# A two-layer attention and gated-MLP kernel: last-stage arithmetic moved from GpSimd to VectorE and ScalarE, weight splits tied to the last attention blocks, gates and first loads reordered

## The chip, the cores and the metric

The kernel runs on one core of a Trainium2 chip. The metric is the device time of one execution in microseconds (us), as the median of three runs. The engines are named as in the profile: PE (TensorE matmuls), PEld (its weight loads), DVE (VectorE), ACT (ScalarE), POOL (GpSimd) and SP (SyncE, which here issues most of the DMAs).

## What is computed

The input is a sequence of 2048 tokens of width 1024 and 256 context tokens. Two layers are applied, each followed by a residual and a layer norm:

```python
def even_layer(x, xc, c, c_ctx, ...):        # layer 0
    q_a, k_a, v_a, g_a, q_b, k_b, v_b, g_b = even_heads(modulate(x, shift, scale) @ w_in, ...)
    # 8 heads with low-rank q and kv (rms norms of rank 384 and 256) and a rope part,
    # 8 heads of 64 with 2 kv heads; keys are context + sequence
    y = attend_and_merge(...)                # softmax attention, times silu(gate), @ w_out
    x_new = layer_norm(ALPHA * x + gate * y, ln_g, ln_b)
def odd_layer(x, ...):                       # layer 1
    u, v, g = jnp.split(modulate(x, shift, scale) @ w_in, 3, axis=-1)
    v = layer_norm(jax.nn.gelu(v), v_ln_g, v_ln_b)
    # v is mixed over chunks of 128 tokens by w_s, then
    y = (jax.nn.gelu(u) * mixed * jax.nn.silu(g)) @ w_out
    x_new = layer_norm(ALPHA * x + gate * y, ln_g, ln_b)
```

All of it is float32. Every product of two matrices is made of three matmuls: each operand is split into a high part `h` (rounded to the type that TensorE reads at full rate) and a low part `l = x - h`, and h·h, h·l and l·h are summed in PSUM. A split is thus one copy with rounding and one subtraction over the tile; the weights are split on the chip too.

## The kernel before

There are three stages on one instruction stream per engine. A planner of the framework orders the instructions of each engine when the kernel is built, by program order as priority and by its own estimate of when each becomes ready; what is emitted under `tc.high_priority()` goes first. On the chip every engine runs its queue in that fixed order and waits on semaphores. In attention the order of PE, DVE, ACT and POOL is written out by hand (class `InOrder`, whose every instruction has line 588 in the profile).

**Stage 1, `phase1`.** First the modulation row: 16 loads of `e_w_mod` (512 KB each) feed matmuls of two rows (L118). The raw tiles of the context and of the first 512-token chunk are loaded between the third and the fourth group of these loads. Then come two halves, the first with the context and chunks 0 and 1, the second with chunks 2 and 3. `acts` scales a chunk's raw tiles on ACT (L165) and splits them on POOL (L167) and DVE (L168); `weights` loads a weight tile of 512 KB and splits it on POOL (L147) and DVE (L148); `gemm` makes 24 matmuls of 512 columns (L176 to L178). The split chunks stand in a ring of nine tile pairs. In each half there are the keys, values and queries of the second kind of head, the low-rank kv part, the low-rank q part (`w1[8]` to `w1[10]`, then a norm over 384 channels, `finish`, which I call the join of the query norm: square sums by a matmul L240, Sqrt L242, reciprocal, multiply, split), and the product with `uq`, which needs the join. The 16 units of the generator `gate` (`gates`, a `gemm`, a Silu L295 and a store to `G`) are put between these parts where the program calls `next(gate)`; what is left of them is run behind `uq`. In the second half those last gates run beside `first_peaks`: 28 units of one product and one row maximum (L603, L607, L617, L620) that find the largest score of each query for the first two attention blocks. The negated maxima of block 0 go to memory (`NM`) and come back as a row of the query tile (`peak_row`), and the first score product of attention reads that row.

**Stage 2, `attention`.** 64 blocks (16 heads by four groups of 512 queries) of 18 key tiles each. POOL adds the exponentials `ph` of most key tiles into a running sum (`sa`), for all blocks but the last four (`shares`); `total` splits the sum on ACT (`sh`) and POOL (`sl`). `sh` stands in ACT's hand-written order among the exponentials of the next block.

**Stage 3, `phase3`.** Four batches of 512 tokens. `even_out` is the out-projection, residual and norm of layer 0, with transposes L970 at its end; `odd_in` is the in-projection of layer 1: `v` (L978, ACT), then 16 column tiles `j`, eight for `u` and eight for `g`; `odd_out` is the last projection (its PSUM tiles are emptied by L1046) with the norm L948 and L949. PSUM tiles `acc` are a ring of six, of which a half of a projection fills four. Weights are split on ACT (L65) and DVE (L66). The first three weight tiles, `pre`, are split on POOL instead (L62, L63, through `split(..., pool=True)`) and may run as soon as they are loaded. For a `g` tile, ACT makes the Silu into an SBUF tile `y` (L1019) and POOL multiplies it into `u` (L1020). POOL also turns the normalized residual `T` into `T * eg + eb` in eight instructions of 128x1024 a batch (L1032), which may run when the transposes have read `T`.

Of the kernel before, what the change touches and what calls it, by code (L numbers as in the profile page):

```python
# [54 lines left out]
    e.eps = e.epsq[1.0]  # L55


def split(e, h, l, src, pool=False):

    if pool:  # L60
        pool = e.nc.gpsimd if pool is True else pool
        pool.tensor_scalar(out=h, in0=src, scalar1=1.0, scalar2=0.0, op0=ALU.mult, op1=ALU.add)  # L62
        pool.tensor_tensor(out=l, in0=src, in1=h.bitcast(F32), op=ALU.subtract)  # L63
    else:
        e.nc.scalar.activation(h, src, AF.Copy)  # L65
        e.nc.vector.tensor_tensor(out=l, in0=src, in1=h.bitcast(F32), op=ALU.subtract)  # L66


def phase1(e):
    nc, tc, I = e.nc, e.tc, e.ins  # L70
    early = ExitStack()
    with tc.tile_pool(name="p1c", bufs=1) as cp, tc.tile_pool(name="p1", bufs=2, reuse_waits="tile") as sp, \
# [28 lines left out]
        def raws(c, kk, tag="xr", bufs=2):  # L101
            src = I["ctxT"] if c < 0 else I["xT"][:, c * CH:(c + 1) * CH]
            src = src.rearrange("(k p) t -> p k t", p=P)
            r = sp.tile([P, 2, CH], F32, name="xr", tag=tag, bufs=bufs)
            nc.sync.dma_start(r[:, :, :CTX if c < 0 else CH], src[:, 2 * kk:2 * kk + 2, :])
            return r
# [4 lines left out]
        for j in range(4):  # L111
            ps = pp.tile([P, CH], F32, name="ps", tag="ps", bufs=5)
            for kk in range(4):
                tag, bufs = ring[(4 * j + kk) % 8]
                w = sp.tile([P, 2, CH], F32, name="wr", tag=tag, bufs=bufs)
                nc.sync.dma_start(w, I["e_w_mod"].rearrange("(k p) f -> p k f", p=P)[:, 2 * kk:2 * kk + 2, j * CH:(j + 1) * CH])
                for k in range(2):
                    nc.tensor.matmul(ps[:2, :], lhsT=sc[:, 2 * kk + k, :], rhs=w[:, k, :],  # L118
                                     start=kk + k == 0, stop=kk + k == 4)
            mrow = ap.tile([2, CH], F32, name="mrow", tag="sq", bufs=4)  # L120
            nc.scalar.activation(mrow, ps[:2, :], AF.Copy)
            for i in range(4):
                nc.tensor.transpose(mps[:, 4 * j + i, :], mrow[:, i * P:(i + 1) * P], e.ident[:2, :2])
            if j == 2:

                raw = {(c, kk): raws(c, kk, "xl", 9) for c in (-1, 0) for kk in range(4)}
        md = cp.tile([P, 2, 16], F32, name="md")
        for c in range(2):
            nc.vector.tensor_tensor(out=md[:, c, :], in0=mps[:, :, c], in1=bmod, op=ALU.add)
# [6 lines left out]
        def weights(src, shape):  # L136
            for f in aside[:rate]:
                f()
            del aside[:rate]
            w = sp.tile([P, 1024], F32, name="wr", tag="wr", bufs=2)  # L140
            n = 1
            for s in shape[1:]:
                n *= s
            nc.sync.dma_start(w[:, :n], src)
            h = sp.tile([P, 1024], F32R, name="wh", tag="wh", bufs=3)
            l = sp.tile([P, 1024], F32R, name="wl", tag="wl", bufs=3)
            nc.gpsimd.tensor_scalar(out=h[:, :n], in0=w[:, :n], scalar1=1.0, scalar2=0.0, op0=ALU.mult, op1=ALU.add)  # L147
            nc.vector.tensor_tensor(out=l[:, :n], in0=w[:, :n], in1=h[:, :n].bitcast(F32), op=ALU.subtract)  # L148
            if len(shape) == 3:
                return tuple(t[:, :n].rearrange("p (a b) -> p a b", a=shape[1]) for t in (h, l))  # L150
            return tuple(t[:, :n].rearrange("p (a b c) -> p a b c", a=shape[1], b=shape[2]) for t in (h, l))
# [128 lines left out]
        for half in range(2):  # L280
# [172 lines left out]

                        queue.append(finish)

            next(gate)
            for s in range(3):
                w = weights(I["uq"][s], [P, 2, 3, P])
                for i in range(2):
# [20 lines left out]
                todo = first_peaks(e, sp, pp)  # L480
            for i, _ in enumerate(gate):
                if half == 1 and i > 0:
                    for f in todo[:7]:
                        f()
                    del todo[:7]
            assert not aside
        flush()
        for f in todo:
# [144 lines left out]
def first_peaks(e, sp, pp):  # L633

    nc, (K, _), Q = e.nc, e.first[0], e.first[1]
    e.stats, pms = {}, {}

    def one(i, m):
        peak_products(e, nc.tensor, pp, pms, (0, i), i, K, Q[i], m, "misc", 3)
        peak_maxima(e, nc.vector, e.kp, pms, e.stats, i, m)  # L640

    return [lambda i=i, m=m: one(i, m) for i, n in ((0, NTT), (1, AHEAD)) for m in range(n)]


def attention(e):
# [8 lines left out]
    with tc.tile_pool(name="atc", bufs=1, reuse_waits="tile") as cp, \  # L654
# [135 lines left out]
        def at(time, *unit):  # L790
            units.append((time, len(units), unit))

        stats.update(e.stats)
        for i in range(NW):
            if i > 1:
                at((i - 2) * NTT + 1.2, fetch_queries, i)
            if i % NG == 1 and i // NG + 1 < 2 * NH:
                at(i * NTT + 1.2, fetch_keys, i // NG + 1)
            for m in range((NTT, AHEAD)[i] if i < 2 else 0, NTT):
                at(i * NTT - NTT - AHEAD + m + 0.6, peak, i, m)  # L800
                at(i * NTT - NTT - AHEAD + m + 1.3, top, i, m)
            at(max(0, i * NTT - AHEAD + 2.5) - (i == 0), row, i)
        for s in range(NW * NTT):
            i, t = divmod(s, NTT)
            parts, adds = shares(i)
# [25 lines left out]
        at(end - (NG - 2) * NTT + 1, lambda: z_load(e, 0, e.Z[0].groups[3]))  # L831
        for k in range(NK):
            at(end - (NG - 1) * NTT + 4 * k + 17, lambda k: z_split(e, e.Z[0][k], sp.tile([P, CH], F32, name="zt", tag="zt", bufs=2), POOL), k)
        for _, _, (f, *args) in sorted(units):
            f(*args)


def phase3(e):
    nc, tc, I = e.nc, e.tc, e.ins
    NB = SEQ // CH  # L840
    with tc.tile_pool(name="p3c", bufs=1, reuse_waits="tile") as cp, \
# [41 lines left out]
        def wtile(q):  # L883
            return wp.tile([P, 1024], F32R if q else F32, name="w" + q, tag="w" + q, bufs=3 if q else 2)

        def weights(src, a, hl=None, w=None, pool=False):
            w = w or wtile("")
            nc.sync.dma_start(w.rearrange("p (a b) -> p a b", a=a), src)
            h, l = hl or (wtile(q) for q in "hl")
            with tc.high_priority():  # L890
                split(e, h, l, w, pool)
            return tuple(t.rearrange("p (a b) -> p a b", a=a) for t in (h, l))

        def residual(b, T, q):
# [80 lines left out]
        def odd_in(b, X, Z, T, v):  # L975
# [28 lines left out]
            for j in range(16):  # L1004
# [7 lines left out]
                if j < 8:  # L1012
                    if j % 2 == 0:
                        u = sp.tile([P, 2, CH], F32, name="u", tag="u", bufs=4)
                        U += [u[:, i, :] for i in range(2)]
                    nc.scalar.activation(U[j], ps, AF.Gelu_apprx_tanh)
                else:
                    y = tmp("y", 3)
                    nc.scalar.activation(y, ps, AF.Silu)  # L1019
                    nc.gpsimd.tensor_tensor(out=U[j - 8], in0=U[j - 8], in1=y, op=ALU.mult)  # L1020
                    if j > 8:
                        gated(j - 9, st)
                    mixed(j - 8, st)
# [5 lines left out]
                        z_load(e, b + 1, Z.groups[j], nc.gpsimd)  # L1029
                if 4 <= j < 12:  # L1030
                    t = (j - 4) // 2
                    nc.gpsimd.tensor_tensor(out=T[:, t, :], in0=T[:, t, :], in1=C["eb" if j % 2 else "eg"], op=ALU.add if j % 2 else ALU.mult)  # L1032
            gated(7, st)
            return U

# [4 lines left out]
        def odd_out(b, Z, T):  # L1040
            xr = [T[:, t, :] for t in range(4)]

            def evac(t, cc, ps):
# [8 lines left out]
            token_major(Z, I["o_w_out"], 0, evac, stagger=b == NB - 1)  # L1052


        pre = [weights(I["e_w_out"].rearrange("(k p) f -> p k f", p=P)[:, 2 * kk:2 * kk + 2, :CH], 2, pool=True)
               for kk in range(3)]
        ge, T = (wp.tile(x, F32, name=n, bufs=1) for n, x in (("gate_e", [P, D]), ("t", [P, 4, D])))
        C["gate_e"] = ge
# [136 lines left out]
```

## Time and profile before

| | before |
|---|---|
| median of 3 runs | 3336.63 us (3332.5 to 3338.37) |
| the profiled execution | 3341.19 us, span of its instructions 3339.4 us |
| PE busy | 3200.2 us, 96% of the span, 13698 matmuls |
| DVE, ACT, POOL busy | 2541.0 (76%), 1890.9 (57%), 1777.9 us (53%) |
| mean granted TensorE clock | 0.984 |

The span runs from the first to the last instruction. Busy is the time in which at least one instruction of the engine ran; matmuls are pipelined, so PE counts as busy whenever they follow each other closely, also at a lower clock.

### The profile page before, as it was taken

The page shows a single profiled execution, that of the slowest core. Times are in us where ns is not written, and L with a number is a line of the kernel's source. Part 1 is how long each engine was busy: PE and PEld are TensorE (multiplying, and loading weights), DVE is VectorE, ACT ScalarE, POOL GpSimd, SP SyncE. Part 2 cuts the span into 40 slices and gives each one's busy share as a digit, 9 for nine tenths or more (in the row PEclk, how much of TensorE's full clock was granted, in tenths as well). Part 3 has the DMA queues.
Part 4 walks back from the last instruction along what each step waited for, and adds up shares of the span by engine and source line. Part 5 has one row for each costly group of instructions (what it writes and reads, how often), then busy time and mean ns, then how long its engine had stood idle before and what let it go on. Part 6 is the DMA issues. An engine that isn't in the chain of part 4 may idle for free.

```text
span 3339.4 us, 40476 instructions
## 1 busy us (share of the span) xinstructions
PE 3200.2 (96%) x13698; PEld 2435.2 (73%) x13698; DVE 2541.0 (76%) x3621; ACT 1890.9 (57%) x3258; POOL 1777.9 (53%) x1423
## 2 busy tenths in 40 slices
PE   7999999989999999999999999999899999899998
PEld 3886777767777777777666666677688788688786
DVE  4847794578988889888999999996745755755746
ACT  3433342257777777777777777776343353353342
POOL 3312431269999999998888888854301301301201
PEclk9999999989999999999999999999999999999999
DMA  6446745552122231222111111113533533533322
GB/s 231 141 163 188 231 146 188 159 124 62 39 49 60 60 65 39 49 60 60 30 28 30 28 43 33 28 29 61 158 94 108 151 95 110 146 97 108 107 89 76
DMA packets 187057, 314.09 MB, mean 94 GB/s; under 512 B 53264, under 2 KB 79184, under 8 KB 184928
## 3 DMA queue, kind: packets, MB, share of 16 engines
q1 hardware_dynamic: 178558, 283.62, 30.2%
q0 software_dynamic: 8000, 27.81, 2.8%
q8 instruction: 108, 1.77, 0.3%
q14 instruction: 101, 0.83, 0.1%
q10 hardware_dynamic: 290, 0.07, 0.0%
HBM read 240.71 MB, written 70.73 MB: 93 GB/s over the span
## 4 chain that ended last, share of the span: by engine, by line
PE 52%; DMA 10%; POOL 8%; DVE 8%; issue 5%; ACT 3%; SPq 0%; POOLq 0%; ACTq 0%; DVEq 0%
PE s L588 12%; POOL sa L588 6%; PE ol L588 6%; DMA NM<-nm 6%; PE oh L588 4%; PE m L588 4%; PE acc L1011 4%; PE acc L1010 4%; PE acc L1009 4%; PE acc L915 3%; PE acc L914 3%; PE acc L916 3%; DVE pl L588 2%; DMA q<-NM 2%; DMA w<-in_o_w_in 1%
## 5 line engine op out<-in xcount | busy, mean ns | idle before, releaser
L588 POOL TENSOR_TENSOR sa<-sa,ph 128x512 f32<-128x512 f32 x728 | 939.7, 1291 | 61.0 <-ACT ph L588 15.5
L588 PE MATMUL s<-q,k 96*128 96x512 f32 (+2 forms) x2880 | 874.3, 400 | 40.8 <-DVE pl L588 22.9
L588 DVE TENSOR_TENSOR pl<-s,ph 128x512 fp32r<-128x512 f32 x1064 | 728.6, 685 | 115.7 <-ACT s L588 93.0
L588 ACT ACTIVATE ph<-s 128x512 fp32r<-128x512 f32 x1064 | 633.7, 596 | 310.8 <-PE s L588 294.1
L588 DVE TENSOR_REDUCE mx<-m 128x1 f32<-128x512 f32 x1124 | 763.7, 682 | 58.7 <-PE m L588 55.2
L588 PEld LDWEIGHTS s<-q,k 96*128 96x128 f32 (+2 forms) x2880 | 538.9, 190 | 253.3 <-DVE pl L588 45.5
L588 ACT ACTIVATE s<-s 128x512 f32<-128x512 f32 x1064 | 632.7, 595 | 0.0
L588 PE MATMUL oh<-ph,v 128*128 128x512 f32 x1152 | 455.5, 395 | 0.0
L588 PE MATMUL ol<-pl,v 128*65 128x512 f32 x1152 | 455.1, 395 | 0.0
L588 PE MATMUL m<-k,q 128*128 128x512 f32 (+1 forms) x1250 | 451.2, 377 | 0.0
L65 ACT ACTIVATE wh<-w 128x1024 fp32r<-128x1024 f32 x153 | 162.2, 1060 | 491.3 <-PE acc L916 219.2
L66 DVE TENSOR_TENSOR wl<-w,wh 128x1024 fp32r<-128x1024 f32 x153 | 202.2, 1321 | 267.6 <-ACT wh L65 266.8
L1020 POOL TENSOR_TENSOR u<-u,y 128x512 f32<-128x512 f32 x32 | 63.6, 1988 | 416.7 <-ACT y L1019 416.7
L588 PEld LDWEIGHTS m<-k,q 128*128 128x128 f32 (+1 forms) x1250 | 234.7, 190 | 67.2 <-DVE mx L588 14.3
L177 PE MATMUL ps<-xl,wh 128*128 128x512 f32 (+1 forms) x640 | 250.3, 391 | 6.9 <-DVE xl L168 6.8
L176 PE MATMUL ps<-xh,wh 128*128 128x512 f32 (+1 forms) x640 | 249.1, 390 | 6.3 <-POOL wh L147 3.4
L588 PEld LDWEIGHTS oh<-ph,v 128*128 128x128 f32 x1152 | 217.9, 189 | 49.5
L178 PE MATMUL ps<-xh,wl 128*128 128x512 f32 (+1 forms) x640 | 248.8, 389 | 1.7 <-DVE wl L148 1.7
L588 PEld LDWEIGHTS ol<-pl,v 128*65 128x65 f32 x1152 | 157.4, 137 | 50.7 <-ACT ob L588 0.3
L914 PE MATMUL acc<-wh,k 128*128 128x512 f32 x384 | 159.7, 416 | 24.1 <-DVE y L1046 18.6
L915 PE MATMUL acc<-wl,k 128*128 128x512 f32 x384 | 158.4, 412 | 8.5 <-DVE wl L66 8.4
L916 PE MATMUL acc<-wh,k 128*128 128x512 f32 x384 | 156.9, 409 | 0.0
(300 smaller groups left out, 5372.5 us busy)
## 6 DMA issues: line engine op xcount, KB each, us to landing
w<-in_wug SPq DMA_DIRECT2D x64, 512.0 KB
wr<-in_w SPq DMA_DIRECT2D x38, 512.0 KB
w<-in_e_w_out SPq DMA_DIRECT2D x32, 512.0 KB
w<-in_o_w_in SPq DMA_DIRECT2D x32, 512.0 KB
w<-in_o_w_out SPq DMA_DIRECT2D x32, 512.0 KB
wr<-in_e_w_mod SPq DMA_DIRECT2D x24, 512.0 KB
wr<-in_o_w_mod SPq DMA_DIRECT2D x24, 512.0 KB
q<-QB SPq DMA_DIRECT2D x96, 128.0 KB
```

Of the source, the lines that this page charges most:

```text
L65: e.nc.scalar.activation(h, src, AF.Copy)
L66: e.nc.vector.tensor_tensor(out=l, in0=src, in1=h.bitcast(F32), op=ALU.subtract)
L176: nc.tensor.matmul(out, lhsT=wh(k), rhs=xh(k), start=i == 0, stop=False)
L177: nc.tensor.matmul(out, lhsT=wh(k), rhs=xl(k), start=False, stop=False)
L178: nc.tensor.matmul(out, lhsT=wl(k), rhs=xh(k), start=False, stop=i == n - 1)
L588: i = getattr(self.engine, name)(*args, **kw)
L914: nc.tensor.matmul(ps[t], lhsT=h[:, ts], rhs=w[0][:, k, :], start=first, stop=False)
L915: nc.tensor.matmul(ps[t], lhsT=h[:, ts], rhs=w[1][:, k, :], start=False, stop=False)
L916: nc.tensor.matmul(ps[t], lhsT=l[:, ts], rhs=w[0][:, k, :], start=False, stop=last)
L1009: nc.tensor.matmul(ps, lhsT=w[0][:, k, :], rhs=h, start=k == 0, stop=False)
L1010: nc.tensor.matmul(ps, lhsT=w[0][:, k, :], rhs=l, start=False, stop=False)
L1011: nc.tensor.matmul(ps, lhsT=w[1][:, k, :], rhs=h, start=False, stop=k == NK - 1)
```

## The change

It has four parts. (1) In stage 3 the Silu is written in place in PSUM, and DVE instead of POOL multiplies it into `u`; the eight instructions on `T` run on DVE instead of POOL. (2) The POOL splits of `pre` get an order edge: they stand behind the POOL instruction that was the last one emitted at the 0th, 5th and 10th key tile of the last attention block. (3) In stage 1, three gates (first half) and two (second half) are called ahead of `uq` instead of one; the peaks are spread 9, 9, then 5 to a gate, with `peak_row` of block 0 behind the first 18 instead of at the start of attention. (4) The loads of `w1[0]` and `w1[1]`, into two tiles of the ring `xh`, are issued ahead of the last four loads of `e_w_mod`, and the raw tiles of chunk 0 behind those.

```diff
-def split(e, h, l, src, pool=False):
+def split(e, h, l, src, pool=False, after=None):
...
-        pool.tensor_scalar(out=h, in0=src, scalar1=1.0, scalar2=0.0, op0=ALU.mult, op1=ALU.add)
+        a = pool.tensor_scalar(out=h, in0=src, scalar1=1.0, scalar2=0.0, op0=ALU.mult, op1=ALU.add)
+        if after:
+            e.tc.add_manual_dep(a.ins, after, mybir.DependencyInfo(mybir.DependencyClass.NoSync, mybir.DependencyReason.DATA))
...
-                raw = {(c, kk): raws(c, kk, "xl", 9) for c in (-1, 0) for kk in range(4)}
+                raw = {(-1, kk): raws(-1, kk, "xl", 9) for kk in range(4)}
+                wpre = []
+                for i in range(2):
+                    w = sp.tile([P, 1024], F32, name="wr", tag="xh", bufs=9)
+                    nc.sync.dma_start(w.rearrange("p (k f) -> p k f", k=NK), I["w1"][i])
+                    wpre.append(w)
+        raw.update({(0, kk): raws(0, kk, "xl", 9) for kk in range(4)})
...
-            next(gate)
+            for _ in range(2 if half else 3):
+                next(gate)
             for s in range(3):
                 w = weights(I["uq"][s], [P, 2, 3, P])
...
             for i, _ in enumerate(gate):
                 if half == 1 and i > 0:
-                    for f in todo[:7]:
+                    n = 9 if i < 3 else 5
+                    if i == 3:
+                        todo.pop()()
+                    for f in todo[:n]:
                         f()
-                    del todo[:7]
+                    del todo[:n]
...
-    return [lambda i=i, m=m: one(i, m) for i, n in ((0, NTT), (1, AHEAD)) for m in range(n)]
+    return [lambda i=i, m=m: one(i, m) for i, n in ((0, NTT), (1, AHEAD)) for m in range(n)] + [lambda: peak_row(e, 0, 0, Q[0])]
...
+        e.marks = []
+        for k in range(3):
+            at(end - NTT + 5 * k, lambda: e.marks.append(POOL.last))
...
-                    y = tmp("y", 3)
-                    nc.scalar.activation(y, ps, AF.Silu)
-                    nc.gpsimd.tensor_tensor(out=U[j - 8], in0=U[j - 8], in1=y, op=ALU.mult)
+                    nc.scalar.activation(ps, ps, AF.Silu)
+                    nc.vector.tensor_tensor(out=U[j - 8], in0=ps, in1=U[j - 8], op=ALU.mult)
...
-                    nc.gpsimd.tensor_tensor(out=T[:, t, :], in0=T[:, t, :], in1=C["eb" if j % 2 else "eg"], op=ALU.add if j % 2 else ALU.mult)
+                    nc.vector.tensor_tensor(out=T[:, t, :], in0=T[:, t, :], in1=C["eb" if j % 2 else "eg"], op=ALU.add if j % 2 else ALU.mult)
...
-        pre = [weights(I["e_w_out"].rearrange("(k p) f -> p k f", p=P)[:, 2 * kk:2 * kk + 2, :CH], 2, pool=True)
+        pre = [weights(I["e_w_out"].rearrange("(k p) f -> p k f", p=P)[:, 2 * kk:2 * kk + 2, :CH], 2, pool=True, after=e.marks[kk])
                for kk in range(3)]
```

## Rows read from the trace of the kernel before

**Rows 1.** Waits of PE: total us, times, longest us.
```profile
PE s L588 <- DVE pl L588: 22.9, 37, 6.9
PE acc L914 <- DVE y L1046: 18.6, 6, 3.9
...
PE acc L915 <- DVE wl L66: 9.1, 2, 8.4
```

**Rows 2.** Stretches: us, busy us (instructions) of each engine, granted clock, DMA.
```profile
core 0: us, PE busy (x) PEld busy (x) DVE busy (x) ACT busy (x) POOL busy (x), PEclk, DMA share, GB/s
40.00:60.00 20.00, 12.06 (x41) 9.19 (x41) 17.12 (x13) 14.72 (x24) 17.84 (x13) 0.66 0.35 119
305.00:326.00 21.00, 13.35 (x35) 5.27 (x34) 19.26 (x18) 9.73 (x15) 3.66 (x3) 0.84 0.35 113
366.00:384.00 18.00, 14.01 (x46) 8.97 (x45) 6.86 (x5) 9.71 (x14) 8.06 (x7) 0.81 0.71 234
596.00:611.00 15.00, 10.10 (x27) 6.65 (x27) 11.95 (x15) 7.15 (x11) 0.43 (x1) 0.77 0.14 52
660.00:692.00 32.00, 23.52 (x86) 17.06 (x85) 21.17 (x36) 5.61 (x9) 1.50 (x2) 0.84 0.88 192
717.00:731.00 14.00, 7.15 (x24) 4.85 (x23) 5.32 (x9) 6.14 (x12) 10.70 (x9) 0.76 0.14 43
1043.70:1148.70 105.00, 104.67 (x458) 80.25 (x457) 93.61 (x153) 79.65 (x150) 97.12 (x79) 1.00 0.24 54
2230.00:2330.00 100.00, 97.79 (x422) 70.37 (x420) 76.80 (x123) 74.07 (x138) 36.05 (x35) 1.00 0.28 52
2400.00:2418.00 18.00, 9.64 (x30) 7.12 (x30) 14.87 (x11) 6.88 (x10) 8.15 (x3) 0.72 0.20 59
2606.00:2622.00 16.00, 10.21 (x31) 7.24 (x30) 16.00 (x11) 1.06 (x1) 14.03 (x5) 0.79 0.12 33
2640.00:2890.00 250.00, 240.53 (x1049) 192.78 (x1048) 158.20 (x189) 99.56 (x135) 49.88 (x36) 0.99 0.39 118
```

**Rows 3.** Timeline of DVE and POOL in the last stage: start, us, instruction.
```profile
2385.94 5.51 POOL L1032 TENSOR_TENSOR t<-t,eg 128x1024 f32<-128x1024 f32 x2
...
2386.30 5.70 DVE L66 TENSOR_TENSOR k<-y,k 128x512 fp32r<-128x512 f32 x2
...
2412.08 1.23 DVE L66 TENSOR_TENSOR wl<-w,wh 128x1024 fp32r<-128x1024 f32 x1 [0.25 <-ACT wh L65]
...
2609.41 0.68 DVE L1046 TENSOR_TENSOR y<-acc,gate_o 128x512 f32<-128x512 f32 x1
```

**Rows 4.** The page's costliest groups: busy us, mean ns | idle before, releaser.
```profile
L588 ACT ACTIVATE s<-s 128x512 f32<-128x512 f32 x1064 | 632.7, 595 | 0.0
...
L1020 POOL TENSOR_TENSOR u<-u,y 128x512 f32<-128x512 f32 x32 | 63.6, 1988 | 416.7 <-ACT y L1019 416.7
```

**Rows 5.** Groups of DVE by line and form, from 2430 us on.
```profile
L1000 DVE TENSOR_TENSOR u<-tp,u 128x512 f32<-128x512 f32 x32 | 22.1, 690 | 67.5 <-PE tp L999 67.5
```

**Rows 6.** Timeline of POOL and ACT in the first attention block.
```profile
697.04 4.76 POOL L63 TENSOR_TENSOR wl<-w,wh 128x1024 fp32r<-128x1024 f32 x2
...
722.40 0.63 ACT L588 ACTIVATE sh<-sa 128x512 fp32r<-128x512 f32 x1 [9.73 <-POOL sa L588]
```

**Rows 7.** Timeline of ACT and PE at the first half's query join.
```profile
301.89 1.28 ACT L242 ACT_TABLE_LOAD   x1 [3.25 <-PE ss L240]
303.19 0.69 ACT L242 ACTIVATE sq<-ss,eps 128x512 f32<-128x512 f32 x1
...
312.98 0.80 PE L240 MATMUL ss<-oq,ones 128*128 128x512 f32 x1 [5.69 <-ACT oq L231]
```

**Rows 8.** The chain that ended last, 640 to 690 us: start, us, what.
```profile
662.01 5.47 DVE mx L617 x9
...
674.43 8.73 DMA NM<-nm
683.17 2.67 DMA q<-NM
```

**Rows 9.** Timeline of PE behind the modulation.
```profile
43.84 0.58 PE L176 MATMUL ps<-xh,wh 128*128 128x256 f32 x1 [3.41 <-POOL wh L147]
```

More of the change, by code (lines that the diff above doesn't have):

```diff
@@ L139, in weights @@
             del aside[:rate]
-            w = sp.tile([P, 1024], F32, name="wr", tag="wr", bufs=2)
             n = 1
@@ L143, in weights @@
                 n *= s
-            nc.sync.dma_start(w[:, :n], src)
+            if wpre:
+                w = wpre.pop(0)
+            else:
+                w = sp.tile([P, 1024], F32, name="wr", tag="wr", bufs=2)
+                nc.sync.dma_start(w[:, :n], src)
             h = sp.tile([P, 1024], F32R, name="wh", tag="wh", bufs=3)
@@ L801, in attention @@
                 at(i * NTT - NTT - AHEAD + m + 1.3, top, i, m)
-            at(max(0, i * NTT - AHEAD + 2.5) - (i == 0), row, i)
+            if i:
+                at(i * NTT - AHEAD + 2.5, row, i)
         for s in range(NW * NTT):
@@ L884, in wtile, with weights @@
             return wp.tile([P, 1024], F32R if q else F32, name="w" + q, tag="w" + q, bufs=3 if q else 2)
-        def weights(src, a, hl=None, w=None, pool=False):
+        def weights(src, a, hl=None, w=None, pool=False, after=None):
             w = w or wtile("")
@@ L890, in weights @@
             with tc.high_priority():
-                split(e, h, l, w, pool)
+                split(e, h, l, w, pool, after)
             return tuple(t.rearrange("p (a b) -> p a b", a=a) for t in (h, l))
```

## The prediction

> **What bounds the kernel now.** I first read the stretches by engine. In the heads of attention PE is dense: 458 matmuls in 105.0 us, 0.229 us each, at the full clock, with nothing left between them although POOL is busy for 97 of these 105 us [rows 2]. So PE's own work sets the time there, and what a change can win lies in the stretches where PE falls short of that rate. I price them all in one way: the length of a stretch less its number of matmuls times 0.229 us. That holds both the idle time and the matmuls that ran at the lower granted clock after it (the share falls to 0.72 in 2400 to 2418 us; the two levels are 1.2 and 2.4 GHz) [rows 2].
>
> Then I read PE's waits, to see who ends them. In the last stage six waits, 18.6 us in all, are ended by the DVE instruction that empties a PSUM tile (L1046), and one of 8.4 us by the low part of a weight; in attention the longest wait for DVE's `pl` is 6.9 us [rows 1]. The timeline of the last stage shows why DVE is late: while POOL runs the eight instructions on `T`, about 2.8 us each, DVE's subtractions of 128x512 between SBUF tiles take 2.85 us each (5.70 for two), against 1.23 us for twice their size when POOL is quiet; the one that reads PSUM takes 0.68 us in the middle of such a burst [rows 3]. The two engines run in lockstep for some 22 us, once a batch.
>
> **Last stage: POOL's arithmetic to DVE.** There are four bursts, and the stretch around the first lost 18.0 - 30 x 0.229 = 11.1 us of PE, that of 2606 to 2622 us 16.0 - 31 x 0.229 = 8.9 us; the two later batch boundaries repeat the latter [rows 2]. Sum: 11.1 + 3 x 8.9 = 37.8 us. Added to DVE: 32 instructions on `T` at 1.23 us (the weight's subtraction, of the same shape) [rows 3] and 32 products with `u` at 0.69 us (L1000, the same shape with one operand in PSUM) [rows 5], 61 us in all. DVE has the room: in a whole batch it is busy 158 of 250 us, stretched instructions included [rows 2]. The Silu in place costs ACT what it cost before, going by the exponential that runs in place in PSUM, 0.595 us [rows 4]. POOL's product of 1.99 us [rows 4] goes, and with it nothing of the path, as no PE wait names it. What comes back: the `T` instructions may run as soon as the transposes are done, in the same places as now, so one may stand ahead of each batch's first PSUM emptying. I charge one per batch, 4 x 1.2 = 4.9 us, and take **33 us**. Lower bound 15 (all eight of a batch, 9.8 us, ahead of the emptying, less the 4 us by which the first of four tiles is complete before the last: 5.8 us lost four times); upper bound 38.
>
> **Splits of the first weights.** In the first attention block POOL makes three splits; two of the subtractions are 4.76 us, between its sums. ACT then waits 9.73 us for the sum of that block, and the next block's exponentials are queued behind `sh` [rows 6]. PE lost 14.0 - 24 x 0.229 = 8.5 us there [rows 2]. Behind the marks the splits run among the last four blocks, which have no sums: POOL is busy 36 of the last 100 us, so some 10 us more fit [rows 2]. Their SP loads: two tiles may still be loaded early; the third load, and the loads of the next weights behind it, now wait for splits that come within the last block. The first needs to be there some 24 us later at the start of stage 3, and the third weight two weights on. I take **8 us**; bounds 3 (a weight is late once) and 9.
>
> **First half, gates ahead of the join.** PE waits 5.69 us for a square sum whose ACT copy is late [rows 7], and 305 to 326 us lost 21.0 - 35 x 0.229 = 13.0 us [rows 2]. Two more gates are 48 matmuls, 11.0 us, of cover: enough for all but a small rest. Their weight load, two Silus and two stores join the SP and ACT queues, where the `uq` weights and the join stand behind them. I take **9 us** of 13; bounds 0 and 13. In return only one gate is left behind `uq`. But the gates that read chunk 0 are then done before `uq`, so chunk 2 can be split during `uq`; today the boundary lost 18.0 - 46 x 0.229 = 7.5 us [rows 2]. I take **3 us**; bounds -4 (the single gate covers too little) and 7.
>
> One cost speaks against this part. Silu and Sqrt need a switch of ACT's function table between them, and in this trace a Sqrt starts 1.30 us after its table load did [rows 7]. If a gate's Silu falls between the Sqrts of the two chunks, a join gets up to two more switches, 2.6 us on its ACT chain; this is within what I leave of the 13 us, and a rival below. The Trainium skill ("ScalarE: Activation LUTs", section "What ACT_TABLE_LOAD costs") puts a switch at some 2.66 us, a load and a drain; by that each join would be 5.3 us later and the sum some 5 us smaller over both. The trace shows no drain there.
>
> **Second half and the start of attention.** The join's stretch lost 15.0 - 27 x 0.229 = 8.8 us [rows 2]; one more gate (5.5 us) covers its idle part. But that gate is missing at the end, where the start of attention hangs on a chain and not on PE: 18 maxima in a row, 0.61 us each where they run freely, then 8.73 us until the maxima are in memory and 2.67 us for the row to come back [rows 8]; the whole stretch already loses 32.0 - 86 x 0.229 = 12.3 us [rows 2]. So the gate's 5.5 us are not saved, only moved: 8.8 - 5.5 = 3.3 us. The earlier `peak_row` is still behind the store, whose landing sets it; ahead of it on SP now stand gate stores. Nine peaks to a gate instead of seven win at most a microsecond. I take **3 us**; bounds -5 and 8.
>
> **First loads.** PE first waits 3.41 us for POOL's copy of `w1[0]` [rows 9], and in 40 to 60 us it is idle for 7.9 us and has a clock share of 0.66 [rows 2]; the matmuls there have two shapes, so I don't use 0.229. With two weights loaded ahead, their POOL and DVE splits can stand before the modulation is ready, out of the way of the activations' splits. DVE and POOL are busy 17.1 and 17.8 of these 20 us [rows 2], so about 7 us of such work gone matters. Against it, chunk 0 now waits behind two weights and four loads of `e_w_mod`, 3 MB more. I take **4 us**; bounds -4 and 9.
>
> **Sum.** 33 + 8 + 9 + 3 + 3 + 4 = 60 us. The profiled execution took 3341.2 us (its span 3339.4 and 1.8 around it); 3341.2 - 60 = 3281 us. The median of the runs lies 4.6 us below that execution, so I put the forecast at **3277 us**.
>
> **Rivals.**
> *Everything clears.* If all six parts come at their upper ends but one or two (the `T` instructions fall where DVE is idle, the half boundary closes), the gain is about 77 us, 3260 us. For it: DVE loses its stretched instructions, more time than it gains. Chance 0.14.
>
> *Stage 1 gives nothing.* Its chains are latencies (loads, the maxima's round trip), and a gate moved ahead is missing behind. Then 60 - 19 = 41 us remain, 3296 us. For it: the 12.3 us at the start of attention. Against: the first join's wait is plainly uncovered. Chance 0.16.
>
> *`T` ahead of the emptying.* The lower bound of the first part everywhere: 15 in place of 33, 3295 us. Chance 0.10.
>
> *Table switches.* Four more loads at 1.30 us, all exposed, and the clock with them, some 9 us: 3286 us. Chance 0.04. The figure of the Trainium skill's page named above would make it some 5 us more.
>
> *DVE waits in order (slower).* The product with `u` waits for a Silu that follows the last matmul of its column tile. If the planner puts it ahead of the next weight's low part, that part comes 0.6 + 0.7 + 1.2 = 2.5 us late, and with the clock about 4 us, up to 32 times: 128 us, 3405 us. It decides from 15 of the 32 on, where the 60 us are eaten. Against it: L1000 stands in that stage today, waits for PE's transposes 67.5 us in all [rows 5], and no PE wait there names DVE. Chance 0.06, of which a third stops near no change.
>
> The forecast itself, between 3266 and 3288 us, has the remaining 0.50. The range, 3254 to 3303 us, reaches over all the faster rivals and leaves out the slower one and tails of the others. Within 0.2% (6.7 us, about what a measurement of this kernel can tell from no change): 0.03. Slower: 0.04. Faster: 0.93.
>
> **What would show it.** Right: no POOL arithmetic after the last block; DVE subtractions at 0.69 and 1.23 us throughout the last stage; no PE wait for L1046 over 1.5 us; no 6.9 us wait in the second attention block, ACT's wait for the first sum under 2 us, and POOL's L63 among the last block's instructions; at the first join PE running gates; the start of attention idle for longer than today. Wrong: DVE waits of a microsecond or more ahead of a weight's low part; the first weights of stage 3 late; X splits of chunk 0 waiting for DMA at 45 us; new PE waits at the half boundary.

## The result, and the profile after

The changed kernel takes 3283.8 us (median of 4 runs, 3280.5 to 3286.7) against 3337.5 us for the kernel before in the same session: a ratio of 0.9838 with an interval of 0.9819 to 0.9857. A second series of the same kernel, in a later session, gave 3280.7 us and 0.9828 (0.9810 to 0.9845). The forecast was 3277 us, a gain of 60; the gain is 54 in the first series and 57 in the second.

The profiled execution took 3284.3 us, its span 3282.5. I split the difference of the spans, 56.9 us, at three instructions of PE that both traces have. The first attention score starts at 680.2 us in place of 686.0: stage 1 is 5.8 us shorter (forecast 9 + 3 + 3 + 4 = 19). From there to the last attention product it is 4.8 us (forecast 8), and from the first matmul of the last stage to the end 46.4 us (forecast 33). So the sum came out nearly right from terms most of which did not: that the last stage gave 13 us more than forecast and stage 1 13 us less is luck.

The waits of PE in the changed kernel, total us, times, longest:

```profile
PE s L603 <- DMA q<-NM: 18.2, 17, 8.9
PE s L603 <- DVE pl L603: 16.4, 32, 1.9
PE ss L251 <- ACT oq L242: 10.1, 5, 6.3
...
PE ps L187 <- POOL xh L178: 6.6, 2, 4.3
...
PE tp L990 <- DVE t L984: 3.4, 1, 3.4
```

All six waits for the instruction that empties a PSUM tile, and the two for a weight's low part, are gone [rows 1]: the last stage has no wait for DVE of half a microsecond or more left but the 3.4 us ahead of its first transposes, which the kernel before has too. The longest wait for `pl` fell from 6.9 to 1.9 us. But a wait of 6.3 us at the first query norms' join is there as before, when it was 5.7 [rows 7], and a wait of 4.3 us for `xh`, at the half boundary, is new: before, the longest of its kind was 1.2 us.

Stretches of the changed kernel (us, length, then busy us and instructions of each engine, granted clock, DMA). They answer to [rows 2], moved to where the same work now lies:

```profile
40.00:60.00 20.00, 13.46 (x55) 10.51 (x55) 15.19 (x13) 14.73 (x24) 17.01 (x12) 0.83 0.37 136
303.00:327.00 24.00, 16.94 (x60) 13.02 (x60) 22.49 (x22) 10.43 (x16) 4.81 (x4) 0.79 0.31 102
366.00:384.00 18.00, 12.92 (x47) 9.55 (x46) 10.22 (x10) 6.77 (x10) 6.00 (x4) 0.81 0.80 260
592.00:607.00 15.00, 13.79 (x61) 10.86 (x60) 12.55 (x16) 7.98 (x13) 0.86 (x2) 1.00 0.36 122
654.00:686.00 32.00, 21.38 (x56) 12.82 (x56) 20.07 (x36) 4.78 (x8) 1.28 (x1) 0.69 0.76 188
711.00:725.00 14.00, 14.00 (x64) 10.79 (x63) 13.29 (x24) 10.74 (x21) 12.58 (x11) 1.00 0.09 19
...
2296.00:2306.00 10.00, 8.08 (x28) 5.43 (x28) 3.85 (x7) 5.79 (x12) 5.71 (x5) 0.83 0.30 87
2312.60:3269.70 957.10, 951.83 (x4193) 766.05 (x4191) 589.14 (x798) 394.64 (x531) 39.64 (x67) 1.00 0.39 118
2385.00:2403.00 18.00, 18.00 (x79) 14.50 (x78) 12.79 (x14) 7.78 (x11) 0.00 (x0) 1.00 0.34 105
2590.00:2606.00 16.00, 16.00 (x71) 12.96 (x70) 13.88 (x16) 2.53 (x3) 4.30 (x7) 1.00 0.67 167
```

In the last two, the first burst and the first batch boundary, PE now runs without a gap at a granted clock of 1.00 (before 0.72 and 0.79). The second and third have hardly gained: 24.0 - 60 x 0.229 = 10.3 us are lost at the first join, 18.0 - 47 x 0.229 = 7.2 us at the half boundary (7.5 before). The 13.0 us of before at the first join are not their like: eight matmuls `rows<-acc,pick`, dearer than 0.229 us, stand inside that window and outside this one. The first four of them before, and all eight in the changed kernel:

```profile
315.26 3.57 PE L273 MATMUL rows<-acc,pick 128*2 128x512 f32 x4
```

```profile
330.21 3.60 PE L284 MATMUL rows<-acc,pick 128*2 128x512 f32 x8
```

At the full clock the eight take 3.60 us, 1.8 us more than 8 x 0.229, so 13.0 - 1.8 = 11.2 us is the loss to compare with 10.3. The last stage of the kernel before up to its last matmul, and two stretches of it that the prediction did not price:

```profile
2655.00:2675.00 20.00, 17.55 (x68) 13.69 (x68) 19.48 (x28) 11.00 (x16) 1.08 (x2) 0.91 0.47 152
2900.00:2925.00 25.00, 21.04 (x81) 15.94 (x81) 22.47 (x33) 11.82 (x18) 1.86 (x4) 0.93 0.59 193
2323.10:3326.70 1003.60, 965.78 (x4193) 773.42 (x4191) 625.32 (x734) 393.72 (x531) 193.14 (x131) 0.98 0.37 112
```

The same 4193 matmuls took 1003.6 us and take 957.1. In the profiles of the splits, the gates and the loads alone (below), where this stage is that of before, they took 998.7, 1002.7 and 999.1 us; so 41.6 to 46.5 us are gained, by the execution that is compared. DVE's busy time there fell from 625 to 589 us although 64 instructions were added to it. The groups of DVE in the last stage, by form (busy us, mean ns | idle before), and two instructions of the first burst show why:

```profile
L68 DVE TENSOR_TENSOR wl<-w,wh 128x1024 fp32r<-128x1024 f32 x153 | 187.0, 1222 | 253.0 <-ACT wh L67 252.0
...
L1039 DVE TENSOR_TENSOR u<-acc,u 128x512 f32<-128x512 f32 x32 | 21.9, 685 | 0.9 <-ACT acc L1038 0.7
```

```profile
2380.21 1.22 DVE L1051 TENSOR_TENSOR t<-t,eb 128x1024 f32<-128x1024 f32 x1
...
2382.60 1.29 DVE L68 TENSOR_TENSOR k<-y,k 128x512 fp32r<-128x512 f32 x2
```

The pair `k<-y,k`, 5.70 us beside POOL's work on `T` [rows 3], takes 1.29 us, and all 153 subtractions of a weight average 1222 ns.

### The profile page after: what moved, and what is told of

Same layout as the page of the kernel before. It is cut to its first block, busy times and chain, and to the rows that moved or that the text cites. A ratio compares the mean times of both kernels' runs of the same rounds, so it can differ in the third digit from the quotient of the medians.

```text
span 3282.5 us, 40436 instructions
## 1 busy us (share of the span) xinstructions
PE 3183.2 (97%) x13698; PEld 2429.2 (74%) x13698; DVE 2501.8 (76%) x3685; ACT 1892.4 (58%) x3258; POOL 1623.6 (49%) x1359
## 4 chain that ended last, share of the span: by engine, by line
PE 52%; issue 11%; DMA 9%; POOL 6%; DVE 6%; ACT 2%; SPq 0%; POOLq 0%; ACTq 0%; DVEq 0%
PE s L603 14%; DMA NM<-nm 6%; PE ol L603 6%; PE oh L603 5%; PE m L603 5%; POOL sa L603 4%; PE acc L935 3%; PE acc L934 3%; PE acc L936 3%; PE acc L1031 3%; PE acc L1030 3%; PE acc L1029 3%; DVE pl L603 2%; DMA q<-NM 2%; PE ps L188 1%
## 5 line engine op out<-in xcount | busy, mean ns | idle before, releaser
L68 DVE TENSOR_TENSOR wl<-w,wh 128x1024 fp32r<-128x1024 f32 x153 | 187.0, 1222 | 253.0 <-ACT wh L67 252.0
L158 POOL TENSOR_SCALAR wh<-wr 128x1024 fp32r<-128x1024 f32 (+1 forms) x48 | 57.4, 1197 | 225.3 <-PE ps L188 116.4
L934 PE MATMUL acc<-wh,k 128*128 128x512 f32 x384 | 153.7, 400 | 0.8 <-ACT t L998 0.8
L936 PE MATMUL acc<-wh,k 128*128 128x512 f32 x384 | 152.6, 398 | 0.0
```

Source lines behind the costliest of these rows:

```text
L934: nc.tensor.matmul(ps[t], lhsT=h[:, ts], rhs=w[0][:, k, :], start=first, stop=False)
L936: nc.tensor.matmul(ps[t], lhsT=l[:, ts], rhs=w[0][:, k, :], start=False, stop=last)
```

## The experiments

All are timed beside the kernel before. Five of them make one part of the change alone in the kernel before; their diffs are hunks of the change. The others change the changed kernel further.

**`T` on DVE alone.** Only the engine of the eight instructions of a batch.

```
-                    nc.gpsimd.tensor_tensor(out=T[:, t, :], in0=T[:, t, :], ...
+                    nc.vector.tensor_tensor(out=T[:, t, :], in0=T[:, t, :], ...
```

> The kernel before, with the eight instructions on T of each batch on DVE and all else as it was. Theory (the bursts of these eight on POOL hold DVE up, and nothing else in the last stage does): nearly all of what the last stage gained, 38 to 46 us faster, the PE waits for L1046 gone. Rival (every POOL instruction of the last stage takes its share, the 32 products with u too): 20 to 28 us faster, and some waits for DVE left.

Measured: 3294.9 us, ratio 0.9875 (0.9861 to 0.9888), so 42 us. Of PE's waits for `acc` the trace shows this one, and none for DVE's emptying or for `wl`; the last stage up to its last matmul stands behind it:

```profile
PE acc L914 <- ACT t L978: 1.0, 1, 1.0
```

```profile
2323.68:3279.30 955.62, 950.23 (x4193) 765.09 (x4191) 597.00 (x767) 393.97 (x531) 104.04 (x99) 1.00 0.39 118
```

The last stage's whole gain comes from this one line: 955.6 us against the 957.1 of the changed kernel.

**Silu in place and the product with `u` alone.**

```
-                    y = tmp("y", 3)
-                    nc.scalar.activation(y, ps, AF.Silu)
-                    nc.gpsimd.tensor_tensor(out=U[j - 8], in0=U[j - 8], in1=y, op=ALU.mult)
+                    nc.scalar.activation(ps, ps, AF.Silu)
+                    nc.vector.tensor_tensor(out=U[j - 8], in0=ps, in1=U[j - 8], op=ALU.mult)
```

> The kernel before, with the Silu in place in PSUM and its product with u on DVE, and T left on POOL. Theory (T's bursts alone cost PE time): within 5 us of the kernel before, all waits for L1046 still there. Rival (the products take their share): 10 to 18 us faster. Second rival (DVE waits in order for the Silu and holds the next weight's low part): slower by 10 us or more.

Measured: 3337.9 us, 0.9996 (0.9984 to 1.0007): no change that can be measured. DVE's waits of before stand:

```profile
PE acc L914 <- DVE y L1045: 17.7, 6, 3.2
```

POOL's product took 1.99 us, 32 times [rows 4], and cost PE nothing that can be measured. It did cost DVE time: DVE's busy time in the last stage is 617.4 us in place of 625.3 although the 22 us of products were added to it.

**The first splits behind the marks, alone.**

```
+        for k in range(3):
+            at(end - NTT + 5 * k, lambda: e.marks.append(POOL.last))
...
-        pre = [weights(..., 2, pool=True)
+        pre = [weights(..., 2, pool=True, after=e.marks[kk])
```

> The kernel before, with only the order edges of the first weight splits. Theory (one stall at the second attention block, and POOL has slack elsewhere in the heads): the 6.9 us wait gone and 8 us less at the second block; of it 3 us come back in waits for the row of maxima or at the end of attention, so 4 to 9 us faster. Rival (POOL bounds all heads of the first kind, so its 10 us of splits count in full): 10 to 12 us faster.

Measured: 3332.7 us, 0.9980 (0.9971 to 0.9989), 6.7 us. The 6.9 us wait in the second block is gone; a new one of 2.2 us for `pl` stands in the last block.

**The gates alone.** Three and two gates ahead of the joins, the peaks dealt out anew, `peak_row` earlier.

```
-            next(gate)
+            for _ in range(2 if half else 3):
+                next(gate)
```

> The kernel before, with only the gates moved ahead of the joins, the peaks spread 9, 9, 5 and the row's load behind the first 18. Theory (in PE's order the moved gates stand behind the second chunk's square sum, so they cannot cover the 6 us wait for it, which is ACT waiting for a load; and at the end the start of attention is a chain of latencies): 0 to 4 us faster, the wait for the square sum in the first half still 5 us or more, the wait for the first score longer than 7.3 us. Rival (the forecast of before): 10 to 15 us faster.

Measured: 3333.2 us, 0.9991 (0.9983 to 1.0000), 3.0 us. The first join still waits 6.1 us for ACT's copy, and a wait of 4.2 us for `xh` is new at the half boundary, where the longest single wait was 1.6 us.

**The first loads alone.** Two weights ahead of chunk 0's raw tiles.

```
-                raw = {(c, kk): raws(c, kk, "xl", 9) for c in (-1, 0) for kk in range(4)}
+                raw = {(-1, kk): raws(-1, kk, "xl", 9) for kk in range(4)}
+                wpre = []
...
```

> The kernel before, with only the first loads reordered. Theory (the two weights are split while PE still makes the modulation; the rest of the opening is set by the activations' splits): first projection matmul 1.5 to 2 us earlier, the low-clock time there down by half, 2 to 4 us kept until attention. Rival (the later raw tiles of chunk 0 give it back): within 1 us of the kernel before at the first score.

Measured: 3336.5 us, 0.9995 (0.9986 to 1.0005). The first projection's matmul starts at 42.9 in place of 43.8 us, less than the theory's 1.5 to 2 us; but the first attention score starts at 681.1 in place of 686.0 us, which is against the rival.

Taken of 3338.8 us, the five ratios give 41.7 + 1.3 + 6.7 + 3.0 + 1.7 = 54.4 us; all parts together gave 54. The parts add up, as far as their intervals tell: half widths of 3 to 4.5 us each leave some 8 us either way for the sum.

**The marks earlier**, in the changed kernel, 11 key tiles of the last heads.

```
-            at(end - NTT + 5 * k, lambda: e.marks.append(POOL.last))
+            at(end - 29 + 5 * k, lambda: e.marks.append(POOL.last))
```

> The changed kernel, with the three marks 11 key tiles earlier (29, 24 and 19 tiles ahead of the end instead of 18, 13 and 8). Theory (the first split on POOL holds up the product of the block before the last, so its sums reach memory late and DVE's reciprocal, in its fixed order, stops the last block's low parts): the PE wait of 1.9 us in the last block gone with the low clock behind it, 2 to 4 us faster than the changed kernel, about 3280 us. Rival (the wait belongs to the last block's own chain): no difference, the wait still there.

Measured: 3279.7 us, 0.9819 (0.9806 to 0.9832). The 1.9 us wait is gone. The lines of SP, DVE and PE show the way it took, first in the changed kernel, then with the marks earlier (start, us, instruction; for SP the us include its wait):

```profile
2284.63 9.18 SPq L908 DMA_DIRECT2D w<-in_e_w_out  x2
2293.86 0.31 SPq L790 DMA_DIRECT2D SU<-ob  x1
...
2298.85 0.55 DVE L799 RECIPROCAL rs<-rs 128x64 f32<-128x64 f32 x1 [3.74 <-DMA rs<-SU]
...
2300.00 0.72 PE L603 MATMUL s<-q,k 128*128 128x512 f32 x2 [1.92 <-DVE pl L603]
```

```profile
2284.94 6.93 SPq L908 DMA_DIRECT2D w<-in_e_w_out  x2
2292.70 0.24 SPq L790 DMA_DIRECT2D SU<-ob  x1
...
2297.55 0.54 DVE L799 RECIPROCAL rs<-rs 128x64 f32<-128x64 f32 x1
```

The lines of SP show it sending in order. In the changed kernel two loads of weights hold it until a buffer is free, when POOL has done a split at 2293.4 us; the row of sums `SU`, which ACT had ready at 2290.2, stands behind them. So `rs` is late, DVE waits for it in order, `pl` waits behind that, and PE last. With earlier marks SP is free at 2291.9, before ACT has the row at 2292.7. POOL's product with the gate, which I had thought to be the late link, runs later than before (2296.7 in place of 2293.3 us) and nothing waits.

**The first head's values later**, behind the two query tiles, in the changed kernel.

```
-        load(e, V[:, :, :2 * DV], e.VA[h])
+            late.append(lambda: load(e, V[:, :, :2 * DV], e.VA[h]))
...
                 e.first = keys(e, 0, late), [queries(e, 0, g) for g in range(2)]
+                for f in late:
+                    f()
```

> The changed kernel, with the load of the first head's values issued behind the two query tiles. Theory (the start of attention is a chain of loads, maxima and the row's round trip; the value load stands ahead of the queries in one DMA queue): the first product of the maxima 4 to 6 us earlier, the first score 3 to 5 us earlier, about 3280 us. Rival (the stores of the queries set it, not the queue): no difference.

Measured: 3286.4 us, 0.9834 (0.9822 to 0.9847): no gain. The chain that ended last at the start of attention and three loads on SP, first of the changed kernel, then with the values later (start, us, what):

```profile
654.83 0.49 PE m L618
...
662.54 0.58 SPq L552 DMA_DIRECT2D k<-KA  x1
...
666.90 9.92 DMA NM<-nm
...
680.20 1.62 PE s L603 x3
```

```profile
643.56 0.56 SPq L555 DMA_DIRECT2D v<-VA  x1
...
652.94 0.24 PE m L624
...
665.46 0.58 SPq L555 DMA_DIRECT2D k<-KA  x1
...
666.13 13.56 DMA NM<-nm
...
682.82 1.62 PE s L609 x3
```

The first product for the maxima starts some 2 us sooner, not 4 to 6, and the row of maxima then takes 13.6 in place of 9.9 us to land. The value load that was moved isn't in the row's way: it goes out at 643.6 us, 22 us ahead of the row. What stands just ahead of the row is the load of the next head's keys (`k<-KA`, 1152 KB), 0.7 us ahead in place of 4.4.

**ACT's order at the first join**, in the changed kernel: the scaling of the next half's raw tiles, which waits for a load, is put behind ACT's last copy of a square sum.

```
+            e.copied = nc.scalar.activation(o[:, 0, :], sq, AF.Copy).ins.name
...
+                    if c >= 2:
+                        tc.add_manual_dep(i.ins, e.copied, ...)
```

> The changed kernel, with an order edge that puts ACT's scaling of the second half's raw tiles behind the copy of the last square sum of the first half. Theory (PE's 6.3 us wait at the first join is ACT standing on a load ahead of that copy, and the gates stand behind it in PE's order): that wait falls below 1 us and the first product with uq starts 6 to 9 us earlier; 4 to 8 us faster in all, as the half boundary may take a part back. Rival (the copy is late for another reason, such as the square sum itself): the wait stays.

Measured: 3279.6 us, 0.9820 (0.9808 to 0.9833). ACT and PE at the join, first in the changed kernel, then in this one:

```profile
309.04 0.81 ACT L176 ACTIVATE xr<-xr,md 128x512 f32<-128x512 f32 x1 [7.27 <-DMA wr<-in_uq]
309.76 0.61 ACT L242 ACTIVATE oq<-sq 128x512 fp32r<-128x512 f32 x1
...
310.43 0.80 PE L251 MATMUL ss<-oq,ones 128*128 128x512 f32 x1 [6.31 <-ACT oq L242]
...
312.57 0.63 PE L187 MATMUL ps<-xh,wh 128*128 128x512 f32 x1
```

```profile
303.37 0.63 ACT L244 ACTIVATE oq<-sq 128x512 fp32r<-128x512 f32 x1 [0.82 <-POOL sq L456]
311.03 1.52 ACT L176 ACTIVATE xr<-xr,md 128x512 f32<-128x512 f32 x2 [7.03 <-DMA wr<-in_uq]
...
305.41 0.50 PE L253 MATMUL ss<-oq,ones 128*128 128x512 f32 x1 [0.28 <-POOL oq L245]
```

The 6.3 us wait is gone, and PE reaches the first `uq` matmul at 316.7 in place of 325.9 us. But the first score starts at 680.2 us in both.

The last four ran together, the first of them the changed kernel itself, with no edit.

> The changed kernel itself, beside the versions of it, so that their differences are read on one chip: 3284 us, between 3280 and 3288. Its first join waits 6.3 us for ACT's copy, its half boundary 4.3 us for POOL's split, its last block 1.9 us.

Measured: 3280.7 us (3277.3 to 3284.5). The three waits are 5.2, 4.1 and 2.1 us in this execution.

**That order, and all four gates of the first half ahead of the join.**

```
-            for _ in range(2 if half else 3):
+            for _ in range(2 if half else 4):
```

> The changed kernel with ACT's scalings of the second half's raw tiles behind the copy that the first join's square sum needs, and with all four gates of the first half in front of that join. Theory: the half boundary waits about 4 us because the last raw tiles of chunk 1's successor can only be loaded when the gate that reads the old chunk has been done behind uq; with no gate left behind uq the loads start some 30 us earlier, the boundary's wait falls from 4.0 to under 1 us, and the kernel takes 3275 us, 4 to 5 us less than with the order alone. Rival: the wait at the boundary is set by the loads' bandwidth and by POOL's splits, not by the gate; the kernel takes 3280 us as with the order alone, and ACT's copy at the join may be late again behind the Silus of the added gate.

Measured: 3280.7 us, 0.9827 (0.9812 to 0.9843). The wait for the raw tile at the half boundary is gone, as the theory said, and two others have come: the waits of PE (total us, times, longest) and the wait at the boundary, on ACT and on PE:

```profile
PE ss L253 <- ACT oq L244: 8.3, 5, 4.3
...
PE ps L189 <- DVE oo L68: 5.7, 4, 2.3
```

```profile
370.36 0.63 ACT L67 ACTIVATE oo<-t 128x512 fp32r<-128x512 f32 x1 [5.44 <-DVE t L228]
...
374.52 0.80 PE L253 MATMUL ss<-oq,bones 128*128 128x512 f32 x1 [4.25 <-ACT oq L244]
```

With the tiles early, their splits fall into `uq`, where PE now waits for DVE, and ACT's copy at the next square sum waits behind DVE's rotation. The theory's mechanism was right, its price wrong: nothing is left of it in the time.

**The earlier marks and ACT's order together.**

> The changed kernel with the marks 11 key tiles earlier and ACT's order at the first join, two edits that touch stretches 1900 us apart. Theory: both remove a wait of PE that sets the end, so their gains (about 4 us each) add up: 3276 us. Rival: what the join's order wins in the first half is given back at the half boundary, which waits for loads, and at the start of attention, whose first score has come at 680.2 us in both; then only the marks' gain is left: 3280 us.

Measured: 3278.4 us, 0.9821 (0.9805 to 0.9836), 2.4 us under the unedited kernel beside it. Both waits are gone, but the unedited kernel's own runs are 7.3 us apart and the intervals overlap, so I can't say that it is faster.

**All three edits.**

> The changed kernel with the earlier marks, ACT's order at the first join and all four gates of the first half in front of that join. Theory: 3271 us (4 us for the marks, 4 for the join, 4 for the half boundary). Rival: the start of attention hangs on loads and on the row's way to memory and back, its first score stays at 680 us whatever the first half wins, and the time is that of the earlier marks alone, 3280 us.

Measured: 3281.1 us, 0.9826 (0.9810 to 0.9843): the rival's time.

## Why the prediction was right in sum and wrong in its terms

**Last stage: right in mechanism, 33 us forecast, 46.5 measured (41.6 to 46.5 by the execution of before, 42 in the time of `T` alone).** The rows looked right: four places, 37.8 us. Two things were off. The 4.9 us charged for `T` instructions in front of the first emptying didn't come: the trace shows them spread between the weights' subtractions, and no wait there. And the term stopped at the waits that name DVE. Some 50 us behind two of the boundaries PE also waited 2.4 and 3.1 us for ACT, and those stretches lost 20.0 - 68 x 0.229 = 4.4 and 25.0 - 81 x 0.229 = 6.5 us. They were DVE's delay handed on through ACT, whose emptying L978 stands in its order behind an instruction that waits for DVE's variances:

```profile
2660.51 0.29 ACT L942 ACTIVATE mv<-mv,eps 128x1 f32<-128x1 f32 x1 [3.75 <-DVE mv L941]
...
2663.28 0.50 PE L914 MATMUL acc<-wh,k 128*128 128x512 f32 x1 [2.45 <-ACT t L978]
```

With nothing but `T` moved, 1.0 us of such waits is left. 37.8 + 4.4 + 6.5 = 48.7 us, near the 46.5 of this pair of profiles. The second of these waits is missing in some other executions of the same stage (that of the splits alone has 2.7 us of them in all), so the agreement is within what executions differ by. The upper bound of 38 had the same gap.

That DVE's subtractions between SBUF tiles are held up beside POOL, and its instruction with an operand in PSUM is not, was read from [rows 3]. The Trainium skill ("SBUF — State Buffer", section "SBUF: two separate sides") has it as a lock: GpSimd and a VectorE instruction with two SBUF inputs share one pair of ports, and the one that starts second waits for the other to end. The trace agrees: 2.85 us beside a POOL instruction of 2.8, 0.69 us with POOL quiet.

**Products with `u`: right.** Charged at nothing in path; alone 0.9996. The slower rival, DVE waiting in order for a Silu, did not come: that group idles 0.9 us in all.

**Splits: right in mechanism, 8 us forecast, 4.8 in the profile (6.7 alone).** The stretch that lost 8.5 us loses nothing now (14.0 us for 64 matmuls). The step that was short is "the third load, and the loads of the next weights behind it, now wait for splits that come within the last block": I asked only when the weights are needed, and not what else stands behind these loads on SP. It was the row of sums, and 2296 to 2306 us loses 10.0 - 28 x 0.229 = 3.6 us. 8.5 - 3.6 = 4.9.

**First join: wrong, 9 us forecast, 0.9 measured.** By the windows it is 11.2 - 10.3; by equal work, PE's 1201st matmul starts 3.2 us sooner than before and its 1403rd, with the same work done in both, 4.1 us. The step that failed is "two more gates are 48 matmuls, 11.0 us, of cover". In PE's order the gates stand behind the second chunk's square sum, the very matmul that waits: it starts at 310.4 us and the gates at 312.6. A matmul covers only a wait that comes after it. Moreover the late copy was no lateness of the norm: ACT stood 7.3 us in front of the scaling of a raw tile whose load had not landed (the line names a load of `uq` that SP sent 0.9 us behind the raw tile's), with the copy next in its order, and with the copy put first the wait went. The trace of before shows the same, right ahead of the copy, so it could have been read there:

```profile
311.60 0.81 ACT L165 ACTIVATE xr<-xr,md 128x512 f32<-128x512 f32 x1 [6.65 <-DMA xr<-in_xT]
```

The 13.0 us that were priced hold 1.8 us that no cover could win, the dearer `rows` matmuls.

**Half boundary: wrong, 3 us forecast, 7.5 - 7.2 = 0.3 measured.** The four short waits there became one of 4.3 us and two of some 0.4. In the two kernels with all gates done before `uq`, the loss moved to DVE's and ACT's work on the same tiles.

**Second join and start of attention: 3 us forecast, about 1 measured.** The gate covers the join as said: 592 to 607 us holds 61 matmuls at a clock of 1.00 where 27 ran before. It is also missing at the end as said: PE waits 8.9 us for the row in place of 7.3, and 654 to 686 us loses 32.0 - 56 x 0.229 = 19.2 us, 6.9 more than before; the join's stretch loses 15.0 - 61 x 0.229 = 1.0, 7.8 less. With the first product for the maxima 6.7 us sooner, the first score is 5.8 us sooner; from the one to the other it takes 25.4 us (24.5 before).

**First loads: 4 us forecast, 1.7 measured in time (-1.7 to 4.7), 3.1 in the profile.** The 401st matmul starts at 122.6 in place of 125.8 us (123.4 with the loads alone), and the clock share of 40 to 60 us is 0.83 in place of 0.66 [rows 2]. The splits of both weights now run ahead of the modulation, and PE waits for the activations instead:

```profile
27.23 1.03 POOL L158 TENSOR_SCALAR wh<-wr 128x1024 fp32r<-128x1024 f32 x1 [26.78 <-DMA wr<-in_w]
...
42.12 0.58 PE L187 MATMUL ps<-xh,wh 128*128 128x256 f32 x1 [2.38 <-POOL xh L178]
```

Its wait fell from 3.4 [rows 9] to 2.4 us: one wait lay right behind the other. With this, stage 1's terms are 0.9 + 0.3 + 0.9 + 3.1 = 5.2 us, and the first score came 5.8 us sooner. The parts alone say where it came from: with the loads alone the first score starts 4.9 us sooner, with the gates alone 1.0. These are single profiles, and executions differ: in the run of the products with `u` alone, whose stage 1 is that of before, it starts 2.0 us sooner. But that most of stage 1's gain came from the loads, and little from the gates, is clear of this.

**The rivals.** "Stage 1 gives nothing" came nearest: 5.8 of its 19 us. The table switches did not come: ACT loads the square root's table 12 times, as before,

```profile
L253 ACT ACT_TABLE_LOAD x12 | 15.4, 1283 | 6.7 <-PE ss L251 6.5
```

because the gates' Silus stand behind both chunks' square roots. Without the last stage's extra 13 us that rival would have been the result: the total was right by luck.

What sets the first score is only in part known. In seven profiles of the changed kernel and its versions, the one with later values left out, it starts between 678.4 and 681.9 us, 23.7 to 26.0 us behind the first product for the maxima, and the row's landing takes longer or shorter. In all 14 profiles, those of before, the parts and the versions, the row can be read back 14.0 to 15.2 us after the load of the next head's keys was issued, whether the row itself went out 0.7 us (values later), 4.3 to 4.4 us (with the gates moved) or 5.8 us (without) behind that load. So the row seems to wait for this load of 1152 KB and not for its own 2 KB; no run puts the row ahead of it, so this is not shown. Whether the earlier marks and ACT's order are worth 2 to 4 us, or nothing, the intervals don't say either, though the traces show both waits gone.

## What to carry to other kernels

A matmul moved ahead covers a wait only if it comes before the awaited instruction in the engine's own order: find the instruction that waits, then what the late engine itself stands on, before pricing the cover. Windows that are compared must hold the same work: here eight dearer matmuls made 1.8 us of a seeming loss, so count to the same matmul in both. When a load is made to wait for a buffer, list what is queued behind it; here it was 3.7 us of a two-kilobyte row. When one engine is late, price the whole stage (length less matmuls at the full rate), not only the waits that name it, since its delay also comes back through others.

## What the runs showed of the hardware

POOL's instructions between SBUF tiles cost DVE more busy time than DVE takes for the same work. The 32 on `T`, some 2.8 us each on POOL and 1.22 us each on DVE (39 us), moved alone, brought DVE's busy time in the last stage from 625.3 to 597.0 us: 67 us of stretched subtractions went. The 32 products with `u`, 22 us on DVE, brought it from 625.3 to 617.4, so 30 us went there too, but PE's waits and the kernel's time stayed as they were. And each stop of PE costs more than its idle time: in the last stage PE's waits of 0.4 us and more fell from 37.4 to 4.9 us in all, by 32.5, while the stage became 46.5 us shorter; the rest, 14.0 us of PE's busy time for the same 4193 matmuls, is matmuls that ran at the lower of the two clock levels behind a wait, as in 2400 to 2418 us at a mean of 0.72 [rows 2].
